# Expert rows of a mixture layer: normalized once ahead and gathered, their outputs added onto the residual rows by the scatter

## The chip, the cores and the metric

One core of one Trainium2 chip runs the whole program in one launch. The metric is device time in microseconds, here the median of several executions. The profile comes from one execution of its own and names five engines: PE (TensorE, matrix products; PEld is its weight load), DVE (VectorE), ACT (ScalarE), POOL (GpSimd) and SP (SyncE, which here only issues transfers). Data move between DRAM and the on-chip memory by DMA, issued by SP or ACT from the hardware queues, or by POOL where a row index decides the address (an indirect DMA: a gather or a scatter).

## The reference, cut to what matters

Two transformer blocks over 512 tokens of 1024 float32 features. The change lies in the end of the second block, which in the reference reads:

```python
h = h + jnp.concatenate([a_out, p_out], axis=-1) @ w_out
h = h + moe(rms_norm_2(h, ffn_norm), w_router, b_router, w_gate, b_gate, w_up, b_up, w_down, b_down)
gate = jax.nn.sigmoid(rms_norm_2(h, ple_gate_norm) @ w_ple_gate)
e = rms_norm_2(p @ w_ple_proj, ple_post_norm)
h = h + gate * e
```

In `moe` each token takes its 4 best of 32 experts (a softmax over the 4 logits gives their gates). An expert has three weights of 1024x1024 with biases: gate and up, clamped, `(up + 1) * gate * sigmoid(1.702 * gate)`, and down. The 4 results, times their gates, are summed into the token's row.

## The kernel before

The first 870 us of the profiled execution are the first block and the attention of the second, and no line of them is touched. What follows has three stages.

**Routing** (`attended_rows`, `route`), a token tile of 128 at a time, in the order 3, 2, 1, 0. The output product is added to the residual rows `hx` on DVE (`add_halves`, L855), ACT issues the store of `hx` to the DRAM tensor `base` (L1382), PE transposes `hx` and multiplies by the router, and a chain of small DVE operations makes the logits `lg` (L1314), the best four, and the table `info`: for each token and expert the row of the output to fill, the gate in two parts, the token and the row's norm in two parts. Beside it ACT and DVE split expert weights that SP loads.

**Experts**, e from 0 to 31, up to 112 tokens each (`CAP`). POOL gathers the tokens' rows of `base` into the one tile `xg` (`gather`, L1422), and normalizes them with two operations of 112x1024 (`normalize`, L1512 by the slot's norm and L1513 by the gain row; for the first expert DVE does it). PE transposes them (`flipped`, L345), ACT and DVE split them into a high and a low part. Each weight of 128x1024 is loaded by SP (L293) into a ring of slots, its high part is cast by ACT (`whi`) and its low part subtracted by DVE (`wlo`, L282). A product is three matmuls, high by high, high by low, low by high (`mm3`, L311, L312, L313), so that an expert is 144 matmuls of 512 columns, 6 for biases, 16 transposes and 4 to pick its slots: 170 instructions of PE. The activation is `gm` on ACT and `uc` on DVE. The down product of expert e-1 runs after gate and up of expert e; ACT scales its result by the gate (`yt`, L1522), and POOL scatters 112 rows of it to `ybuf` in DRAM (L1523), which holds four rows a token. Each scatter waits for the landing of the one before it.

**Last stage**, again by token tiles, after a branch (L1652) that is taken only where an expert has over 112 tokens, which does not happen here. SP loads the tile's row of `base` (`hk`), its four rows of `ybuf` (`yb`) and the embedding's rows (`ee`); DVE and POOL add the four rows to `hk` (L1703, L1705, L1706); PE transposes `hk` and multiplies by the gate's weights, loaded in eight parts `w_pg` (`gate_part`, L1576), six of them ahead of the branch. `keep_warm` puts products that nothing reads on PE, 30 behind the last down product and 24 behind the branch (L361).

A scheduler sets the order of the instructions on each engine from the dependencies, and an engine executes its own in that order.

Of the kernel before, what the change touches and what calls it, by code (L numbers as in the profile page):

```python
# [21 lines left out]
P = 128  # L22
# [93 lines left out]
class Plan:  # L116
    """Which of a set of equal slots holds each raw part of the weights, and its high and low parts.

    A stage is the parts that are multiplied at the same time, in the order of their loads: "p" is split into
    two slots, "r" is only read. ahead: how many parts are split before their stage. added: slots that come  # L120
    with a stage, behind the free ones, or from stage early on in front of them; until: the last stage of
    the slots of a pool."""

    def __init__(self, stages, slots, ahead, added=None, until=None, early=0):
# [8 lines left out]
        class State:  # L133
            # slots of each part, free slots in the order of their release, parts loaded and split
# [27 lines left out]
            def begin(st, u):  # L162
                # the splits of a stage and of those ahead of it
# [16 lines left out]
            def goes_on(st, u):  # L180
                # whether the next stages can be split without waits for their slots
# [32 lines left out]
class Piece:  # L214
    """High and low parts of columns of weights, a slot to 1024 columns."""
# [9 lines left out]
def build(tc, I, out, dbg=None, stop=None):  # L225
# [3 lines left out]
    with es:  # L229
# [28 lines left out]
        def ps_mm():  # L258
            # two banks, from one of three pairs in turn
# [17 lines left out]
        def hold(ins, after):  # L277
            # behind another instruction of its engine
# [60 lines left out]
        def transposed(xh, xT, sl, m=P, step=4):  # L339
            # [token, feature] -> feature-major high and low parts  # L340
# [16 lines left out]
        def keep_warm(n, a, b, after=None):  # L357
            # products that nothing reads: they hold the tensor engine's clock up while it has to wait
# [6 lines left out]
        # ------------------------------------------------ first block: mixer  # L365
# [24 lines left out]
        with pool("n0", 2, side="right") as n0:  # L390
# [4 lines left out]
            # values of the selected and the window branch go with the tiles of x  # L395
# [8 lines left out]
            # the gates' columns go with them  # L404
# [81 lines left out]
        def make_blocks(j, t):  # L486
# [14 lines left out]
            # high parts in the columns up to 64, low parts in those behind  # L501
# [98 lines left out]
        # branch gates  # L600
# [17 lines left out]
        with pool("gm", side="right") as gp:  # L618
            # gated mlp: its second half, normalized and mixed over the tokens of a chunk
# [40 lines left out]
        def mlp_tile(tt):  # L660
            # first half of the gated mlp, a token tile
# [208 lines left out]
        def residual_norm(pl, g_post, g_pre, h_src, h_dst, then):  # L870
            # h + rms(product), and its rms -> then(tt, h, xh)
# [27 lines left out]
        # the per-layer embedding's projection, normalized  # L899
# [36 lines left out]
        # ------------------------------------------------ first block: feed-forward  # L936
        trig = const.tile([P, 2, NT, 8], F32, name="trig")
        with pool("rope") as rp:
# [9 lines left out]
            for j, shift in enumerate((0.25, 0.0)):  # L948
                # trig[:, 0] cosine, trig[:, 1] sine, of the angle less a multiple of two pi
# [66 lines left out]
        # ------------------------------------------------ second block: mixer  # L1016
# [17 lines left out]
        # pooled half  # L1034
# [43 lines left out]
        # queries, keys and values: weights a piece ahead, work by token tiles  # L1078
# [96 lines left out]
        def diff_unit(h, qt):  # L1175
# [23 lines left out]
            def second(acc):  # L1199
# [14 lines left out]
                if h == 3 or qt == 0:  # L1214
                    # feature-major
# [36 lines left out]
        # ------------------------------------------------ second block: output product, router  # L1252
# [332 lines left out]
        for k in range(6):  # L1585
            gate_part(k)
# [160 lines left out]
```

## Time and profile before

| What | us |
|---|---|
| median of 3 runs | 2257.14 (2255.09 to 2259.49) |
| span of the profiled execution | 2253.2 |
| PE busy | 2165.2 (96%) |
| DVE busy | 1784.2 (79%) |
| ACT busy | 1374.4 (61%) |
| POOL busy | 531.7 (24%) |

The span runs from the first to the last instruction of the program in the profile; the median is 3.9 us longer. Matmuls overlap, so PE's busy time also covers short waits. In a row of the timeline the number in square brackets is the idle time of the engine just ahead of the instruction, with the instruction that ended it.

### The profile page before, as it was taken

The page shows a single profiled execution, that of the slowest core. Times are in us where ns is not written, and L with a number is a line of the kernel's source. Part 1 is how long each engine was busy: PE and PEld are TensorE (multiplying, and loading weights), DVE is VectorE, ACT ScalarE, POOL GpSimd, SP SyncE. Part 2 cuts the span into 40 slices and gives each one's busy share as a digit, 9 for nine tenths or more (in the row PEclk, how much of TensorE's full clock was granted, in tenths as well). Part 3 has the DMA queues.
Part 4 walks back from the last instruction along what each step waited for, and adds up shares of the span by engine and source line. Part 5 has one row for each costly group of instructions (what it writes and reads, how often), then busy time and mean ns, then how long its engine had stood idle before and what let it go on. Part 6 is the DMA issues. An engine that isn't in the chain of part 4 may idle for free. (4 is left out here: it accounts for less than half of the span.)

```text
span 2253.2 us, 30487 instructions
## 1 busy us (share of the span) xinstructions
PE 2165.2 (96%) x10458; PEld 1655.0 (73%) x10459; DVE 1784.2 (79%) x2583; ACT 1374.4 (61%) x1875; POOL 531.7 (24%) x391
## 2 busy tenths in 40 slices
PE   9999999999999889899999999999999999999998
PEld 7777788888888777667777777776666666666666
DVE  6688772223667676899999999999898898988876
ACT  5666652223554553577777777777676776766753
POOL 0000110000002432423131413133343533514102
PEclk9999999999999999899999999999999999999999
DMA  5411744334653036799999999999899898898836
GB/s 208 149 29 49 254 151 130 100 102 161 203 185 99 29 113 232 245 349 332 362 329 363 330 358 339 350 331 333 308 333 345 291 343 318 319 334 298 311 118 230
DMA packets 164110, 550.07 MB, mean 244 GB/s; under 512 B 23139, under 2 KB 28259, under 8 KB 163948
## 3 DMA queue, kind: packets, MB, share of 16 engines
q1 hardware_dynamic: 143520, 509.01, 63.3%
q10 hardware_dynamic: 12236, 22.25, 2.9%
q0 software_dynamic: 8192, 16.79, 2.3%
q8 instruction: 84, 1.38, 0.3%
q14 instruction: 78, 0.64, 0.1%
HBM read 534.32 MB, written 26.23 MB: 249 GB/s over the span
## 5 line engine op out<-in xcount | busy, mean ns | idle before, releaser
L282 DVE TENSOR_TENSOR wlo<-wraw,whi 128x1024 fp32r<-128x1024 f32 x923 | 1160.8, 1300 | 195.4 <-ACT whi L282 188.3
L282 ACT CAST whi<-wraw 128x1024 fp32r<-128x1024 f32 x923 | 955.4, 1053 | 389.6 <-PE pa L313 123.6
L312 PE MATMUL pa<-wlo,he 128*112 128x512 f32 x504 | 202.5, 402 | 19.8 <-DVE wlo L282 19.8
L312 PE MATMUL pb<-wlo,xe 128*112 128x512 f32 x512 | 210.3, 411 | 6.7 <-DVE wlo L282 6.4
L313 PE MATMUL pb<-whi,xe 128*112 128x512 f32 x512 | 201.3, 394 | 0.0
L313 PE MATMUL pa<-whi,he 128*112 128x512 f32 x504 | 198.2, 393 | 0.0
L311 PE MATMUL pa<-whi,he 128*112 128x512 f32 x504 | 188.9, 395 | 1.2 <-ACT he L282 1.2
L311 PE MATMUL pb<-whi,xe 128*112 128x512 f32 x512 | 186.9, 395 | 0.0
L1513 POOL TENSOR_TENSOR xg<-xg,g_ffn_norm 112x1024 f32<-112x1024 f32 x31 | 180.0, 5806 | 2.6
L1512 POOL TENSOR_SCALAR xg<-xg,slot_norm 112x1024 f32<-112x1024 f32 x31 | 141.1, 4551 | 157.8 <-DMA xg<-base,gi 157.8
L1422 POOL DMA_INDIRECT xg<-base,gi x32 | 34.2, 1069 | 608.5 <-DVE uc L1554 314.2
L317 POOL TENSOR_SCALAR rstd<-ss 128x1 f32<-128x1 f32 (+1 forms) x68 | 25.1, 369 | 622.6 <-DVE ss L862 387.3
L312 PEld LDWEIGHTS pa<-wlo,he 128*112 128x112 f32 x504 | 87.9, 174 | 57.1 <-DVE wlo L282 28.5
L312 PEld LDWEIGHTS pb<-wlo,xe 128*112 128x112 f32 x512 | 89.5, 175 | 46.1 <-DVE wlo L282 14.7
L311 PEld LDWEIGHTS pa<-whi,he 128*112 128x112 f32 x504 | 87.8, 174 | 34.9 <-ACT whi L282 4.9
L311 PEld LDWEIGHTS pb<-whi,xe 128*112 128x112 f32 x512 | 89.6, 175 | 29.5
L312 PE MATMUL pa<-wlo,xe 128*112 128x512 f32 x264 | 107.6, 407 | 2.6 <-DVE wlo L282 2.6
L311 PE MATMUL pa<-whi,xe 128*112 128x512 f32 x264 | 107.5, 407 | 0.0
L313 PEld LDWEIGHTS pb<-whi,xe 128*112 128x112 f32 x512 | 89.5, 175 | 23.6
L313 PEld LDWEIGHTS pa<-whi,he 128*112 128x112 f32 x504 | 87.9, 174 | 25.4
L313 PE MATMUL pa<-whi,xe 128*112 128x512 f32 x264 | 103.9, 394 | 0.1
L313 PE MATMUL po<-whi,xe 128*112 128x512 f32 x248 | 97.8, 394 | 0.0
(588 smaller groups left out, 4665.2 us busy)
## 6 DMA issues: line engine op xcount, KB each, us to landing
wraw<-in_we_gate_dram SPq DMA_DIRECT2D x256, 512.0 KB, 5.6
wraw<-in_we_up_dram SPq DMA_DIRECT2D x256, 512.0 KB, 5.8
wraw<-in_we_down_dram SPq DMA_DIRECT2D x256, 512.0 KB, 5.5
wraw<-in_w_gu_dram SPq DMA_DIRECT2D x44, 512.0 KB, 3.7
wraw<-in_w_down_dram SPq DMA_DIRECT2D x44, 512.0 KB, 4.3
wraw<-in_w_out_dram SPq DMA_DIRECT2D x24, 512.0 KB, 6.0
yb<-ybuf SPq DMA_DIRECT2D x6, 1024.0 KB, 12.5
wraw<-in_w_v_dram SPq DMA_DIRECT2D x10, 512.0 KB, 4.0
```

Of the source, the lines that this page charges most:

```text
L282: return nc.scalar.copy(hi, src), nc.vector.tensor_tensor(out=lo, in0=src, in1=hi.bitcast(F32), op=ALU.subtract)
L311: nc.tensor.matmul(o, a[0], b[0], start=start, stop=False)
L312: nc.tensor.matmul(o, a[0], b[1], start=False, stop=False)
L313: W["mm"] = nc.tensor.matmul(o, a[1], b[0], start=False, stop=stop)
L317: ins = nc.gpsimd.tensor_scalar(out=r[:, :w], in0=ss, scalar1=1.0 / n, scalar2=eps, op0=ALU.mult, op1=ALU.add)
L1422: nc.gpsimd.indirect_dma_start(out=xg[:CAP], out_offset=None, in_=base, in_offset=bass.IndirectOffsetOnAxis(ap=slots[e][1] if ap is None e ...
L1512: nc.gpsimd.tensor_scalar(out=xg[:CAP], in0=xg[:CAP], scalar1=slots[e][3], scalar2=None, op0=ALU.mult)
L1513: nc.gpsimd.tensor_tensor(out=xg[:CAP], in0=xg[:CAP], in1=gpre[:CAP], op=ALU.mult)
```

## The change

1. In `route` the operations that made the row of `ybuf` are gone (`e2`, `rk`, `row`), and the columns of `info` move up by one. At the end of each tile's routing DVE multiplies `hx` in place by its norm and the gain row, and ACT issues its store to a new DRAM tensor `normed`.
2. The gathers of experts 1 to 31 read `normed`, and POOL's two operations an expert are gone. Expert 0 still reads `base` and is normalized on DVE.
3. The scatter adds its rows onto `base` (an indirect DMA with an addition), in place of filling rows of `ybuf`.
4. The last stage loads `hk` in two halves and `ee` for all four tiles, without `yb` and without the additions. All eight parts of `w_pg` are loaded ahead of the branch, and the first tile's transposes go four to a group, before two.

The rest of the diff removes comments and fits the branch that is not taken.

```diff
-        ybuf = dram.tile([4 * S, D], F32, name="ybuf")
+        normed = dram.tile([S, D], F32, name="normed")
...
             if len(seen) == NT:
                 first_rows()
-            e2 = rp.tile([P, 4, NE], F32, tag="eq2", name="eq2", bufs=1)
-            nc.vector.tensor_tensor(out=e2, in0=eq, in1=row[:, tt, :, None].to_broadcast([P, 4, NE]), op=ALU.mult)
-            rk = rp.tile([P, NE], F32, tag="rk", name="rk", bufs=2)
-            nc.vector.reduce_sum(rk, e2.rearrange("p k e -> p e k"), axis=AX)
-            nc.vector.tensor_copy(info[:, tt, :, 0], rk)
...
+            scale_rows(hx, hx, r, gpre)
+            nc.scalar.dma_start(normed[tok(tt), :], hx)
...
         def gather(e, ap=None):
-            nc.gpsimd.indirect_dma_start(out=xg[:CAP], out_offset=None, in_=base, in_offset=bass.IndirectOffsetOnAxis(ap=slots[e][1] if ap is None else ap, axis=0),
+            nc.gpsimd.indirect_dma_start(out=xg[:CAP], out_offset=None, in_=normed if e else base, in_offset=bass.IndirectOffsetOnAxis(ap=slots[e][1] if ap is None else ap, axis=0),
...
-        def normalize(e):
-            if e == 0:
-                for cs in (slice(0, 512), slice(512, D)):
-                    scale_rows(xg[:CAP, cs], xg[:CAP, cs], slots[e][3], gpre[:CAP, cs])
-            else:
-                nc.gpsimd.tensor_scalar(out=xg[:CAP], in0=xg[:CAP], scalar1=slots[e][3], scalar2=None, op0=ALU.mult)
-                nc.gpsimd.tensor_tensor(out=xg[:CAP], in0=xg[:CAP], in1=gpre[:CAP], op=ALU.mult)
+        def normalize_first():
+            for cs in (slice(0, 512), slice(512, D)):
+                scale_rows(xg[:CAP, cs], xg[:CAP, cs], slots[0][2], gpre[:CAP, cs])
+
+        def add_rows(y_, ap):
+
+            nc.gpsimd.indirect_dma_start(out=base, out_offset=bass.IndirectOffsetOnAxis(ap=ap, axis=0), in_=y_, in_offset=None,
+                                         bounds_check=S - 1, oob_is_err=False, compute_op=ALU.add)
...
-            nc.gpsimd.indirect_dma_start(out=ybuf, out_offset=bass.IndirectOffsetOnAxis(ap=slots[e][2], axis=0), in_=yt, in_offset=None,
-                                         bounds_check=4 * S - 1, oob_is_err=False)
+            add_rows(yt, slots[e][1])
...
-                if kp == 1 and e + 1 < NE:
-                    normalize(e + 1)
...
-        nc.sync.dma_start(hs[0], base[tok(0), :])
...
-        for k in range(6):
+        for k in range(8):
             gate_part(k)
...
-            load_rows(0, 4)
...
+            for tt in range(NT):
+                for cs in (slice(0, 512), slice(512, D)):
+                    nc.sync.dma_start(hs[tt][:, cs], base[tok(tt), cs])
+                es.append(wp.tile([P, D], F32, name="ee", bufs=NT))
+                nc.sync.dma_start(es[tt], ed[tok(tt), :])
...
-                for cs in cols:
-                    for z in range(2):
-                        nc.vector.tensor_tensor(out=h[:, cs], in0=h[:, cs], in1=yb[:, z, cs], op=ALU.add)
-                    eng = nc.gpsimd if tt else nc.vector
-                    eng.tensor_tensor(out=yb[:, 2, cs], in0=yb[:, 2, cs], in1=yb[:, 3, cs], op=ALU.add)
-                    nc.vector.tensor_tensor(out=h[:, cs], in0=h[:, cs], in1=yb[:, 2, cs], op=ALU.add)
-                transposed(h, xT, slice(0, P), step=8 // max(parts, 2))
+                transposed(h, xT, slice(0, P), step=4)
```

On DVE, at tile 1 of the routing (`pb` is the output product that is added to this tile's residual), before:

```order
1046 L1352 TENSOR_TENSOR info<-gg,info 128x32
1047 L1318 MAX_INDEX ix<-top,lg 128x8
1048 L1342 TENSOR_SCALAR nm<-top 128x1
1049 L1320 CAST ixf<-ix 128x4
1050 L1322 TENSOR_TENSOR eq<-iota,ixf 128x128
1051 L855 TENSOR_TENSOR hx<-hx,pb 128x512
1052 L1324 TENSOR_REDUCE m<-eq 128x32
1053 L1337 TENSOR_TENSOR eq_8774<-eq,row 128x128
```

and after:

```order
1042 L1344 TENSOR_TENSOR info<-gg,info 128x32
1043 L337 SCALAR_TENSOR_TENSOR hx<-hx,rstd,g_ffn_norm_8125 128x1024
1044 L1311 SCALAR_TENSOR_TENSOR lg<-po,rstd,g_b_router_8114 128x32
1045 L855 TENSOR_TENSOR hx<-hx,pb 128x512
1046 L1314 MAX top<-lg 128x8
1047 L855 TENSOR_TENSOR hx<-hx,pb 128x512
1048 L1315 MAX_INDEX ix<-top,lg 128x8
```

The scaling in place of tile 2 (L337) now stands ahead of the additions of tile 1 (L855); it waits for the landing of tile 2's store to `base`. Tile 3's scaling stands likewise ahead of tile 2's additions, tile 1's ahead of tile 0's, and tile 0's own stands between the MAX and the MAX_INDEX of tile 0.

On POOL, the first three experts, before:

```order
252 L1422 DMA xg<-base,gi_8977 112x1024
253 L1422 DMA xg<-base,gi 112x1024
254 L1512 TENSOR_SCALAR xg<-xg,slot_norm 112x1024
255 L1513 TENSOR_TENSOR xg<-xg,g_ffn_norm_8128 112x1024
256 L1422 DMA xg<-base,gi 112x1024
```

and after:

```order
252 L1418 DMA xg<-base,gi_8965 112x1024
253 L1418 DMA xg<-normed,gi 112x1024 x3
254 L1509 DMA base<-yt,gi 512x1024
255 L1418 DMA xg<-normed,gi 112x1024
256 L1509 DMA base<-yt,gi 512x1024
```

From then on POOL has only a gather and a scatter an expert.

On SP, behind the branch (the loads of the last stage), before:

```order
568 L1668 DMA yb<-ybuf 128x4x256 x4
569 L1576 DMA wraw<-in_w_pg_dram 128x1024 x2
570 L1668 DMA hk<-base 128x1024
571 L1668 DMA yb<-ybuf 128x4x512 x2
572 L1668 DMA ee<-ed 128x1024
573 L1668 DMA hk<-base 128x1024
574 L1668 DMA yb<-ybuf 128x4x512 x2
```

and after:

```order
566 L1655 DMA hk<-base 128x512 x2
567 L1657 DMA ee<-ed 128x1024
568 L1655 DMA hk<-base 128x512 x2
569 L1657 DMA ee<-ed 128x1024
570 L1655 DMA hk<-base 128x512 x2
```

The first load of the stage is now the tile's own row, 256 KB a half, and every `hk` load comes behind the last scatters.

## Rows read from the trace of the kernel before

**Rows 1.** Busy time of each engine in two stretches of the experts; columns on top.

```profile
core 0: us, PE busy (x) PEld busy (x) DVE busy (x) ACT busy (x) POOL busy (x), PEclk, DMA share, GB/s
1200.00:1400.00 200.00, 198.70 (x902) 145.21 (x901) 196.32 (x212) 149.97 (x164) 56.40 (x22) 1.00 0.94 343
1600.00:1800.00 200.00, 192.74 (x839) 135.09 (x838) 178.94 (x199) 140.56 (x154) 76.90 (x21) 1.00 0.91 323
```

**Rows 2.** Groups of DVE and POOL, 960 to 2160: busy, mean ns, idle before.

```profile
L282 DVE TENSOR_TENSOR wlo<-wraw,whi 128x1024 fp32r<-128x1024 f32 x734 | 929.9, 1316 | 13.6 <-ACT whi L282 8.7 <-DMA wraw<-in_we_up_dram 2.1 <-DMA wraw<-in_we_gate_dram 0.3
L1555 DVE SCALAR_TENSOR_TENSOR uc<-uc,gm 112x1024 f32<-112x1024 f32 x31 | 37.7, 1216 | 0.0
...
L1513 POOL TENSOR_TENSOR xg<-xg,g_ffn_norm 112x1024 f32<-112x1024 f32 x29 | 168.0, 5794 | 2.4
L1512 POOL TENSOR_SCALAR xg<-xg,slot_norm 112x1024 f32<-112x1024 f32 x29 | 134.2, 4628 | 147.2 <-DMA xg<-base,gi 147.2
```

**Rows 3.** The same DVE group in the last expert, 2113 to 2160.

```profile
L282 DVE TENSOR_TENSOR wlo<-wraw,whi 128x1024 fp32r<-128x1024 f32 x29 | 33.8, 1218 | 1.5 <-ACT whi L282 1.5
```

**Rows 4.** Timeline, DVE and POOL at 1175: start us, us, instruction.

```profile
1174.70 4.54 DVE L282 TENSOR_TENSOR wlo<-wraw,whi 128x1024 fp32r<-128x1024 f32 x2
...
1175.53 2.64 POOL L1513 TENSOR_TENSOR xg<-xg,g_ffn_norm 112x1024 f32<-112x1024 f32 x1
```

**Rows 5.** Timeline of PE: six stalls in the experts, one with the matmul ahead.

```profile
959.46 0.49 PE L312 MATMUL pb<-wlo,xe 128*112 128x512 f32 x1 [1.96 <-DVE wlo L282]
...
993.02 0.49 PE L312 MATMUL pb<-wlo,xe 128*112 128x512 f32 x1 [1.08 <-DVE wlo L282]
...
1182.02 0.40 PE L311 MATMUL pb<-whi,xe 128*112 128x512 f32 x1
1182.63 0.48 PE L312 MATMUL pb<-wlo,xe 128*112 128x512 f32 x1 [0.21 <-DVE wlo L282]
...
1750.30 0.49 PE L312 MATMUL pa<-wlo,he 128*112 128x512 f32 x1 [0.65 <-DVE wlo L282]
...
1764.92 0.49 PE L312 MATMUL pa<-wlo,xe 128*112 128x512 f32 x1 [0.15 <-DVE wlo L282]
...
2001.70 0.49 PE L312 MATMUL pa<-wlo,he 128*112 128x512 f32 x1 [1.66 <-DVE wlo L282]
```

**Rows 6.** Timeline of DVE in the routing: additions of tiles 2 and 1, one reduction.

```profile
877.57 1.38 DVE L855 TENSOR_TENSOR hx<-hx,pa 128x512 f32<-128x512 f32 x2 [0.77 <-PE pa L313]
...
890.02 0.68 DVE L855 TENSOR_TENSOR hx<-hx,pb 128x512 f32<-128x512 f32 x1
...
905.25 0.37 DVE L1339 TENSOR_REDUCE rk<-eq 128x32 f32<-128x128 f32 x1
```

**Rows 7.** Stores to base issued at 878.98, 890.73 and 898.05: KB, us to landing.

```profile
base<-hx ACTq DMA_DIRECT2D x1, 512.0 KB, 9.4
...
base<-hx ACTq DMA_DIRECT2D x1, 512.0 KB, 8.5
...
base<-hx ACTq DMA_DIRECT2D x1, 512.0 KB, 2.6
```

**Rows 8.** Timeline of POOL: the first expert's gather.

```profile
908.60 1.57 POOL L1422 DMA_INDIRECT xg<-base,gi  x1 [7.41 <-DVE most L1360]
```

**Rows 9.** Scatters, us to landing: the last one, and those from 960 to 2160.

```profile
ybuf<-yt,si POOLq DMA_INDIRECT x1, 3.7
...
ybuf<-yt,si POOLq DMA_INDIRECT x30, 7.2
```

**Rows 10.** Timeline of PE in the last stage: warm products, first matmuls of tiles.

```profile
2188.14 5.72 PE L361 MATMUL tr<-whi 128*128 128x512 f32 x24 [1.41 <-PEq L1652]
...
2194.98 0.50 PE L311 MATMUL pb<-whi,x4T 128*128 128x512 f32 x1 [0.46 <-ACT x4T L282]
...
2223.75 0.50 PE L311 MATMUL pa<-whi,x4T 128*128 128x512 f32 x1 [1.56 <-ACT x4T L282]
...
2236.39 0.50 PE L311 MATMUL pb<-whi,x4T 128*128 128x512 f32 x1 [0.38 <-ACT x4T L282]
```

More of the change, by code (lines that the diff above doesn't have):

```diff
@@ L1259, in build @@
         nc.vector.tensor_copy(iota, iota_i)
-        row_i = mixq.tile([P, NT, 4], I32, name="row_i")
-        row = mixq.tile([P, NT, 4], F32, name="row")
-        nc.gpsimd.iota(row_i, pattern=[[4 * P, NT], [1, 4]], base=0, channel_multiplier=4)
-        nc.vector.tensor_copy(row, row_i)
         tok1_i = mixq.tile([P, NT], I32, name="tok1_i")
@@ L1429, in first_rows @@
             for tt in range(NT):
-                nc.tensor.matmul(pt[:CAP, 0:2], oh0[0][:, tt], info[:, tt, 0, 3:5], start=tt == 0, stop=tt == NT - 1)
+                nc.tensor.matmul(pt[:CAP, 0:2], oh0[0][:, tt], info[:, tt, 0, 2:4], start=tt == 0, stop=tt == NT - 1)
             gi = early.tile([P, 2], I32, name="gi0", bufs=1)[:CAP]
@@ L1528, in build @@
         held = (W["gate"], first)
-        normalize(0)
+        normalize_first()
         prepare_slots(1, 1)
@@ L1569, in build, with gate_part @@
         hs = [row_tile("hk") for _ in range(NT)]
[L1570 removed]
         wpg = []
[L1573 removed]
+        def gate_part(k):
             slot, *pair = W["plan"].next()
             raw = slot_tile(slot, F32, "wraw")
[L1576 to L1578 removed]
+            nc.sync.dma_start(raw, I["w_pg"][k // 2][:, (k % 2) * D:(k % 2 + 1) * D])
             hi, lo = [slot_tile(t, F32R, n) for t, n in zip(pair, ("whi", "wlo"))]
@@ L1661, in build @@
         with pool("fin", 2, side="right") as wp:
-            yv = ybuf.rearrange("(t k) d -> t k d", k=4)
             keep_warm(24, wpg[0][0][:, 0:P], wpg[0][0][:, 0:512])
-            es, ybs = {}, {}
-            chain = []
-            def load(dst, src):
-                ins = nc.sync.dma_start(dst, src)
-                if chain and len(chain) < 9:
-                    hold(ins, chain[-1])
-                chain.append(ins)
-            def load_rows(tt, parts):
-                ybs[tt] = wp.tile([P, 4, D], F32, name="yb")
-                for c in range(parts):
-                    cs = slice(c * D // parts, (c + 1) * D // parts)
-                    load(ybs[tt][:, :, cs], yv[tok(tt), :, cs])
@@ L1679, in load_row @@
-            def load_row(tiles, tt, src):
-                if tt not in tiles:
-                    tiles[tt] = wp.tile([P, D], F32, name="ee")
-                load(tiles[tt], src[tok(tt), :])
-            load_rows(0, 4)
-            for k in range(6, 8):
-                gate_part(k, chain[-1])
-            hs = dict(enumerate(hs))
-            load_row(hs, 1, base)
-            load_rows(1, 2)
-            load_row(es, 0, ed)
-            for tt in range(NT):
-                parts = 4 if tt == 0 else 2
-                cols = [slice(c * D // parts, (c + 1) * D // parts) for c in range(parts)]
-                if tt + 2 < NT:
-                    load_row(hs, tt + 2, base)
-                    load_rows(tt + 2, 2)
-                if tt + 1 < NT:
-                    load_row(es, tt + 1, ed)
-                h, e, yb = hs[tt], es[tt], ybs[tt]
-                xT = [wp.tile([P, 8, P], F32R, name=f"x4T{j}") for j in range(2)]
-                for cs in cols:
-                    for z in range(2):
-                        nc.vector.tensor_tensor(out=h[:, cs], in0=h[:, cs], in1=yb[:, z, cs], op=ALU.add)
-                    eng = nc.gpsimd if tt else nc.vector
-                    eng.tensor_tensor(out=yb[:, 2, cs], in0=yb[:, 2, cs], in1=yb[:, 3, cs], op=ALU.add)
-                    nc.vector.tensor_tensor(out=h[:, cs], in0=h[:, cs], in1=yb[:, 2, cs], op=ALU.add)
-                transposed(h, xT, slice(0, P), step=8 // max(parts, 2))
```

47 lines of the change are left out of this document (22 added, 25 removed).

## The prediction, made before the changed kernel was run

> **What bounds the kernel now.** I read the busy times by stretch first. The experts, from about 940 to 2180 us, are over half of the span, and they run in two regimes [rows 1]. Between 1200 and 1400 PE is busy for 198.70 of 200 us with 902 matmuls; an expert of 170 instructions takes 170 x 200 / 902 = 37.7 us, and no engine but PE can set that. DVE stands beside it with 196.32 us, so it has hardly any slack of its own. Between 1600 and 1800 PE has 192.74 us and 839 matmuls, which is 40.5 us an expert, although DVE has only 178.94. So the second regime loses some 2.8 us an expert to the order of the instructions, not to anyone's total work. Second I read the timeline of PE for its stalls: each ends on `wlo`, the low part that DVE makes [rows 5]. Third I asked what makes `wlo` late. Over all experts one takes 1316 ns in the mean [rows 2], in the last expert, which has no normalization of POOL beside it, 1218 ns [rows 3]. At 1174.70 two of them take 4.54 us where two alone would take 2.44, and POOL's L1513 of 2.64 us lies beside them [rows 4]. POOL's two operations therefore cost DVE (1316 - 1218) x 734 = 72 us over 29 experts, 2.5 us each. DVE time is not the bound; what counts is the PE stall that it leads to.
>
> **The change part by part.**
>
> *POOL's normalization, removed.* I go by stalls, since PE is the bound. In the first regime one stall an expert falls behind the blocked pair: the matmul at 1182.63 starts 0.61 us after the one ahead, where the pitch of all instructions is 198.70 / 902 = 0.22 and I take 0.23 for a full matmul; 0.38 us lost, 0.21 of it shown as idle, so a stall costs some 0.17 more than its idle time [rows 1, 5]. There are 11 such experts, with nearly the same stall, from 1068.8 to 1448.4: -4.2 us. In the second regime most of the loss is not POOL's: at 1750.30 PE waits 0.65 us for a `wlo` that stands on DVE behind the activation `uc`, and there the order is unchanged. What POOL does there is the stall at 1764.92, 0.15 of idle and so 0.32 lost; 13 experts, -4.2. One expert of this regime has a stall of 1.66 at 2001.70 beside POOL; -1.7. The first experts have two large ones, 1.96 at 959.46 and 1.08 at 993.02; -3.0 if both are POOL's, -1.1 if the first is also a late weight. POOL's removed time itself (5.79 + 4.63 us an expert [rows 2]) is off the path and counts for nothing. The gather then feeds the transposes directly and only has more time. The order of PE turns into the second regime one expert earlier: between 0 and +2.8, I take half, +1.3. Sum of the experts: -11.8, between -5 and -17.
>
> *The Trainium skill, "SBUF — State Buffer", section "Who interferes with whom", has a rule for this: a DVE instruction with two inputs there and a GpSimd instruction that reads it exclude each other, and the second is blocked until the first ends. By the rule DVE would lose all of POOL's 10.4 us an expert. The trace has 2.5 us, so it agrees only in part, and the rows decide the sum; by the rule the sum would be that of the second rival below, 2233.8.*
>
> *Scaling in place and second store in the routing, added.* Four scalings of 128x1024, near in kind to `uc` (1216 ns [rows 2]), and four more stores of 512 KB on ACT's queue. The point is where they stand on DVE: in order ahead of the next tile's additions, and waiting for the landing of that tile's own store to `base`, which is read from the same rows. Queued behind the waiting instruction on DVE are the additions, the routing chain and the splits; behind its store on ACT stand the next tile's store to `base` and the exponentials. Step by step: tile 3's scaling delays tile 2's additions, which ended at 878.95, by 1.2 to 2; their store goes at about 880.5 in place of 878.98. It lands 9.4 later [rows 7] at 889.9; tile 2's scaling ends at 891.1; tile 1's two additions of 0.69 with two small operations between end at 892.9, before at 890.70 [rows 6]: +2.2. That store takes 8.5 (901.4), tile 1's scaling ends at 902.7, tile 0's additions at 904.4 against a store at 898.05: +6.3. If it lands in 2.6 as the last one did [rows 7], this wait falls away and +2.2 stays; I take 8.5, since it is the time of the store at the same place. Tile 0's own scaling stands inside its routing chain, +1.2, while three small operations leave it, the longest 0.37 [rows 6], about -0.8 as an estimate. Its store, landing in 2.6, is done by then; in 8.5 it would hold the chain for some 4 more. So the first gather, at 908.60 [rows 8], is late by 6.5, between +2.5 and +10.5. PE has nothing to do before it, and the ring of split weights is full, so nothing later pays it back.
>
> *Scatter that adds.* No row shows an accumulating transfer. In the experts it is hidden: a scatter lands in 7.2 us [rows 9], the next waits for it an expert, 37.7 us, later, and its source rows have further buffers. At the end the last scatter is issued ahead of the branch, so before 2188.14 - 1.41 = 2186.7, and a plain one lands in 3.7 [rows 9, 10], by 2190.4; warm products hold PE until 2193.86 in any case. Twice the time would expose 0 to 3 us. I take 0, since a row of 112 tokens is small, and keep +3.
>
> *The Trainium skill, "DMA: Bandwidth & Descriptors", section "Rules for kernel authors", speaks against this part: an accumulating DMA reads its destination and writes it later, and nothing holds the bytes in between. By it the loads of `hk` cannot pass the last scatter, and each row crosses twice. No run here shows it; by that rule the sum would move by the +3 just named.*
>
> *Last stage.* 8 MB of `yb` loads and all additions go. The start cannot move forward, as the 24 warm products run from 2188.14 for 5.72 us [rows 10]; eight transposes ahead of the first matmul in place of two make it about 0.4 later. The first two tiles take 2223.75 - 2194.98 = 28.8 us, the third 12.64 [rows 10]; with the adds gone both should run like the third: 2 x 12.64 = 25.3, so -3.5. Together -3.1, between 0 and -5. The two more gate parts ahead of the branch are split by ACT and DVE while PE runs the warm products, and their cover is that wait; without it they would cost two `wlo`, 2.4 us.
>
> **Sum.** +6.5 - 11.8 - 3.1 = -8.4. The profiled execution would have a span of 2244.8 in place of 2253.2; the median lies 3.9 above the span, so 2248.7.
>
> **The rivals.**
>
> *No relief.* The stalls of PE come from the order on DVE alone, as at 1750.30 [rows 5], and when POOL is gone another wait for `wlo` stands there. For: DVE has 196.32 of 200 us in the first regime [rows 1]. Against: the last expert without POOL has shorter splits [rows 3]. Then +6.5 + 1.3 - 3.1 = +4.7: 2261.8.
>
> *Full relief.* DVE, freed of 2.5 us or more, runs ahead so far that the second regime loses no idle time of PE: 7.26 of 200 us, 1.47 an expert, 13 experts, -19 in place of -4.2 [rows 1]. Then 2233.8. Against: `uc` waits for PE whatever POOL does.
>
> *Stores behind stores (slower).* On ACT's queue each store to `base` now follows a store to `normed` of the same size. If the two share the queue's time, a landing takes 9.4 longer at tiles 2 and 1, and DVE waits each time: +18.8, net +10.4, 2267.5. It decides from 4.2 us more a landing, where the gain is gone. For: 9.4 and 8.5 show a loaded DMA. Against: 2.6 for the last one [rows 7].
>
> *Accumulating scatter as the bound (slower).* The DMA share is 0.94 in the first regime [rows 1], 6% or 2.3 us an expert free. If an adding scatter takes the engines 7.2 us longer, 4.9 us an expert would show, 31 times: +152, 2401. It decides at 2.3 us.
>
> **How the numbers follow.** Chances: the forecast 0.50, no relief 0.18, full relief 0.10, stores behind stores 0.14, the scatter 0.08 (half of it only the +3 of the end). A measurement tells about 0.2%, 4.5 us, from no change. The forecast with its own spread is faster by that in 0.40 and the same in 0.10; full relief is faster; no relief stands at the edge, 0.12 same, 0.06 slower; stores 0.03 and 0.11; scatter 0.03 and 0.05. So faster 0.50, same 0.28, slower 0.22. The range 2236 to 2266 reaches from near full relief to nearly the slow stores and leaves out the bad scatter.
>
> **What would show it.** Right: `wlo` at 1.22 in the mean, no stall of PE above 0.3 where L1512 stood, first regime at 37.3 us an expert, first gather at 915, tiles of the last stage 12.6 apart. Wrong: a first gather near 909 or beyond 920, stalls of PE that stay, landings of scatters above 15 us, or a second regime that begins elsewhere.

## The result

The changed kernel takes 2236.43 us (median of 4 runs, 2233.82 to 2238.70) against 2257.89 us before (median of 4 runs): a ratio of 0.9906, with a 95% interval of 0.9892 to 0.9920. It is 21.5 us faster, where 8.4 were forecast. The direction was right and the size was not. The time lies 0.4 us inside the lower end of the range. One execution each of two later kernels, of 5307.8 and 3457.2 us, is left out of their times below.

The span of the profiled execution is 2235.0 us, 18.2 less than before. The 3 us between this and the medians lie between executions. A span is some 1.7 us shorter than the time of its execution (2235.0 and 2236.76 here), so the profiled one of before took about 2255 us, 2.9 below its median, and this one lies 0.3 above. I cut the span at the first and the last activation of the experts, the `gm` row on ACT.

Before, the timeline of ACT (start, length, instruction):

```profile
943.58 1.06 ACT L1553 ACTIVATE gm<-gm 112x1024 f32<-112x1024 f32 x1 [0.40 <-DVE gm L1552]
...
2152.20 1.06 ACT L1553 ACTIVATE gm<-gm 112x1024 f32<-112x1024 f32 x1 [4.94 <-DVE gm L1552]
```

After, the same two:

```profile
945.18 1.06 ACT L1547 ACTIVATE gm<-gm 112x1024 f32<-112x1024 f32 x1
...
2133.70 1.06 ACT L1547 ACTIVATE gm<-gm 112x1024 f32<-112x1024 f32 x1 [4.96 <-DVE gm L1546]
```

| Stretch | before | after | moved | forecast |
|---|---|---|---|---|
| up to the first activation | 943.6 | 945.2 | +1.6 | +6.5 |
| first to last activation | 1208.6 | 1188.5 | -20.1 | -11.8 |
| last activation to the end | 101.0 | 101.3 | +0.3 | -3.1 |
| span | 2253.2 | 2235.0 | -18.2 | -8.4 |

In these two executions all of the gain lies in the experts. The page of the changed kernel, its busy times and its costliest group:

```profile
PE 2156.0 (96%) x10458; PEld 1658.2 (74%) x10459; DVE 1699.7 (76%) x2475; ACT 1372.4 (61%) x1873; POOL 199.2 (9%) x323
...
L282 DVE TENSOR_TENSOR wlo<-wraw,whi 128x1024 fp32r<-128x1024 f32 x923 | 1096.7, 1221 | 226.7 <-ACT whi L282 209.8
```

The low part `wlo` takes 1221 ns in the mean over the whole kernel, which is what it took alone [rows 3]. By stretch:

```profile
core 0: us, PE busy (x) PEld busy (x) DVE busy (x) ACT busy (x) POOL busy (x), PEclk, DMA share, GB/s
1200.00:1400.00 200.00, 200.00 (x909) 147.46 (x908) 186.96 (x202) 152.85 (x167) 13.90 (x11) 1.00 0.95 347
1600.00:1800.00 200.00, 193.67 (x851) 137.17 (x850) 172.28 (x190) 142.06 (x156) 12.42 (x10) 1.00 0.91 327
```

In the first regime PE is busy for all of the 200 us and gets through 909 instructions in place of 902; in the second it is 851 in place of 839 [rows 1]. Where the stall stood that delayed a matmul to 0.61 us behind the one ahead [rows 5], 21.3 us behind the activation, PE's timeline now reads:

```profile
1177.42 0.40 PE L313 MATMUL pb<-whi,xe 128*112 128x512 f32 x1
1177.66 0.39 PE L311 MATMUL pb<-whi,xe 128*112 128x512 f32 x1
1177.89 0.40 PE L312 MATMUL pb<-wlo,xe 128*112 128x512 f32 x1
1178.12 0.39 PE L313 MATMUL pb<-whi,xe 128*112 128x512 f32 x1
```

The pitch, the time from start to start, is 0.23 us throughout. In the routing the forecast waits are there, on DVE:

```profile
877.47 1.29 DVE L337 SCALAR_TENSOR_TENSOR hx<-hx,rstd,g_ffn_norm 128x1024 f32<-128x1024 f32 x1 [1.15 <-DMA base<-hx]
...
888.03 1.28 DVE L337 SCALAR_TENSOR_TENSOR hx<-hx,rstd,g_ffn_norm 128x1024 f32<-128x1024 f32 x1 [2.75 <-DMA base<-hx]
...
898.33 1.28 DVE L337 SCALAR_TENSOR_TENSOR hx<-hx,rstd,g_ffn_norm 128x1024 f32<-128x1024 f32 x1 [2.77 <-DMA base<-hx]
```

Each scaling waits for the landing of its tile's store, and the first gather goes at 913.65 on POOL, 5.05 us later than before [rows 8]:

```profile
913.65 1.28 POOL L1418 DMA_INDIRECT xg<-base,gi  x1 [9.31 <-DVE gi L1430]
```

### The profile page after: what moved, and what is told of

It is laid out like the page before. It is cut to its first block, busy times and chain, and to the rows that moved or that the text cites. A ratio compares the mean times of both kernels' runs of the same rounds, so it can differ in the third digit from the quotient of the medians.

```text
span 2235.0 us, 30297 instructions
## 1 busy us (share of the span) xinstructions
PE 2156.0 (96%) x10458; PEld 1658.2 (74%) x10459; DVE 1699.7 (76%) x2475; ACT 1372.4 (61%) x1873; POOL 199.2 (9%) x323
## 5 line engine op out<-in xcount | busy, mean ns | idle before, releaser
L282 DVE TENSOR_TENSOR wlo<-wraw,whi 128x1024 fp32r<-128x1024 f32 x923 | 1096.7, 1221 | 226.7 <-ACT whi L282 209.8
L1509 POOL DMA_INDIRECT base<-yt,gi x32 | 47.7, 1489 | 567.7 <-DVE wlo L282 461.9
L313 PE MATMUL po<-whi,xe 128*112 128x512 f32 x248 | 97.7, 394 | 0.0
L312 PE MATMUL po<-wlo,xe 128*112 128x512 f32 x248 | 97.6, 394 | 0.0
L311 PE MATMUL po<-whi,xe 128*112 128x512 f32 x248 | 97.4, 393 | 0.0
L1418 POOL DMA_INDIRECT xg<-normed,gi x31 | 33.5, 1081 | 600.0 <-PE tr L345 570.2
```

Source lines behind the costliest of these rows:

```text
L282: return nc.scalar.copy(hi, src), nc.vector.tensor_tensor(out=lo, in0=src, in1=hi.bitcast(F32), op=ALU.subtract)
L311: nc.tensor.matmul(o, a[0], b[0], start=start, stop=False)
L312: nc.tensor.matmul(o, a[0], b[1], start=False, stop=False)
L313: W["mm"] = nc.tensor.matmul(o, a[1], b[0], start=False, stop=stop)
L1418: nc.gpsimd.indirect_dma_start(out=xg[:CAP], out_offset=None, in_=normed if e else base, in_offset=bass.IndirectOffsetOnAxis(ap=slots[e][1 ...
L1509: nc.gpsimd.indirect_dma_start(out=base, out_offset=bass.IndirectOffsetOnAxis(ap=ap, axis=0), in_=y_, in_offset=None, bounds_check=S - 1, ...
```

## The theories and the experiments

Three questions were open. Why did the experts gain 20 us and not 12: POOL's operations alone (A), or the order of PE's instructions, which changed in some experts (C)? The sizes of the forecast are B. Why did a gather that is 5 us late cost only 1.6? And where did the last stage's gain go?

**POOL's two operations left out of the kernel before.** Nothing else is changed, and the matmuls stand in the order of before.

```diff
-                nc.gpsimd.tensor_scalar(out=xg[:CAP], in0=xg[:CAP], scalar1=slots[e][3], scalar2=None, op0=ALU.mult)
-                nc.gpsimd.tensor_tensor(out=xg[:CAP], in0=xg[:CAP], in1=gpre[:CAP], op=ALU.mult)
+                pass
```

> The kernel before, with POOL's two operations an expert (L1512, L1513) left out and nothing else: experts 1 to 31 then work on rows that are not normalized, so this part of the computation is missing. The order of the matmuls is that of before, expert by expert. Theory A, POOL's reads block DVE's splits and each late split stops PE: from the first activation of an expert to the last the time falls from 1208.6 us by 18 to 20, as in the changed kernel (1188.6), and the wide stalls of PE ahead of a low part (0.61 us in the first regime, 0.55 in the second, 1.96 and 1.08 in the first experts, 1.66 at 2001) are gone. Theory B, the sizes of the prediction: about -12. Theory C, what changed the experts is the other order of the instructions in the changed kernel: -4 or less.

Measured: 2236.41 us, ratio 0.9903 (0.9876 to 0.9929). Its two activations on ACT:

```profile
943.92 1.06 ACT L1552 ACTIVATE gm<-gm 112x1024 f32<-112x1024 f32 x1
...
2132.47 1.06 ACT L1552 ACTIVATE gm<-gm 112x1024 f32<-112x1024 f32 x1 [4.94 <-DVE gm L1551]
```

The experts take 1188.55 us, as in the changed kernel, though the order is that of before. Theory A holds to a tenth of a microsecond, C falls, and so do the sizes of the forecast (B). The changed kernel also has two small DVE operations an expert fewer, `slot_norm` and `si`, of some 0.15 us each; this kernel still has both, so they are worth nothing that shows.

**The two operations put back into the changed kernel**, first both, then each alone.

```diff
+                if kp == 1 and e + 1 < NE:
+                    nc.gpsimd.tensor_scalar(out=xg[:CAP], in0=xg[:CAP], scalar1=1.0, scalar2=None, op0=ALU.mult)
+                    nc.gpsimd.tensor_tensor(out=xg[:CAP], in0=xg[:CAP], in1=gpre[:CAP], op=ALU.mult)
```

> The changed kernel, with two operations of POOL back at their old place, on the gathered rows: a multiplication by 1.0 and one by the gain row (so the gain is applied twice, which is the only change of the computation). The order of the matmuls is that of the changed kernel. Theory A: the experts take 1188.6 + 18 to 20 us again, and the whole some 18 to 20 us more than the changed kernel. Theory B: +12. Theory C (order): +4 or less.

> The changed kernel, with one operation of POOL an expert back, the multiplication by 1.0 (one tensor read, one written); the result is that of the changed kernel. With both operations back the experts took 1224.7 us, against 1188.5 without. Theory F: what blocks DVE is POOL's operation with two tensors read; this one alone costs 0 to 5 us over the experts. Theory G: any operation of POOL that reads costs by its length; this one has about half of the 36 us.

> The changed kernel, with the other operation of POOL an expert back, the product with the gain row (two tensors read), so that the gain is applied twice. Theory F: 15 to 36 us over the experts against 1188.5. Theory G: about half of the 36 us, 12 to 20. Under both the stall of PE is largest where the operation lies beside the splits that follow the activation.

| Kernel | experts, us | time, us |
|---|---|---|
| changed kernel | 1188.5 | 2236.4 |
| multiplication by 1.0 back | 1195.7 | 2244.6 (one run) |
| product with the gain row back | 1224.4 | 2273.0 (one run) |
| both back | 1224.7 | 2274.6 (2259.0 to 2287.8) |

Both operations back cost 36 us, not the 18 to 20 that A expected from the kernel before: the direction held, the size did not. The costs of the two do not add up either, and the kernel's runs scatter by 29 us. The product with the gain row alone has nearly all of it, as F said, so G falls; the multiplication costs 7, a little more than F's 0 to 5 and all of it in the second regime. The place of the blocked instruction explains most of this. In the kernel with the product back, at 1754, on POOL, DVE and PE:

```profile
1754.04 3.94 POOL L1544 TENSOR_TENSOR xg<-xg,g_ffn_norm 112x1024 f32<-112x1024 f32 x1 [4.02 <-DMA xg<-normed,gi]
...
1754.52 1.21 DVE L282 TENSOR_TENSOR wlo<-wraw,whi 128x1024 fp32r<-128x1024 f32 x1
1755.65 3.42 DVE L1551 SCALAR_TENSOR_TENSOR uc<-uc,gm 112x1024 f32<-112x1024 f32 x1
...
1759.75 1.10 PE L345 MATMUL tr<-ident,uc 112*128 112x112 f32 x8 [2.31 <-DVE xe L282]
```

POOL's operation does not slow the split beside which it begins; the next one, the activation `uc`, takes 3.42 us in place of 1.22, until 1.1 us behind the end of POOL's, and PE, which has its transposes right behind, stands for 2.31. In the kernel with the multiplication back, at 1702:

```profile
1701.64 2.96 POOL L1544 TENSOR_SCALAR xg<-xg 112x1024 f32<-112x1024 f32 x1 [5.35 <-DMA xg<-normed,gi]
...
1701.89 2.06 DVE L1551 SCALAR_TENSOR_TENSOR uc<-uc,gm 112x1024 f32<-112x1024 f32 x1
...
1704.63 1.11 PE L345 MATMUL tr<-ident,uc 112*128 112x112 f32 x8 [0.95 <-DVE xe L282]
```

Here `uc` takes 2.06 and ends at 1703.95, ahead of POOL's end at 1704.60. So one DVE operation an instruction of POOL is held, for about 2.2 us by the product of two tensors and 0.85 by the multiplication by a number, and the price is set by what PE waits for at that moment: 0 where a split has lead, 0.4 to 0.5 in the first regime, over 2 where `uc` is hit. The gather's landing decides which one is hit, as it releases POOL. The one expert of before with 1.66 us at 2001.70 [rows 5] is the same thing, not an accident. There POOL's multiplication starts 5.4 us behind the activation, in the experts next to it 3.5 and 3.7, and the product holds the third `wlo` behind the splits `xe`, so that these four take 7.07 us:

```profile
1995.71 7.07 DVE L282 TENSOR_TENSOR wlo<-wraw,whi 128x1024 fp32r<-128x1024 f32 x4
...
1997.92 2.65 POOL L1513 TENSOR_TENSOR xg<-xg,g_ffn_norm 112x1024 f32<-112x1024 f32 x1
```

A part of the 36 us is the clock and not the block itself. Behind the stall at 1759.75 PE's granted clock (the column behind POOL's) fell to its lower level, 1.2 GHz, in the kernel with the product back:

```profile
core 0: us, PE busy (x) PEld busy (x) DVE busy (x) ACT busy (x) POOL busy (x), PEclk, DMA share, GB/s
1757.00:1759.00 2.00, 0.44 (x2) 0.00 (x0) 2.00 (x2) 1.30 (x2) 0.99 (x1) 1.00 0.62 238
1763.00:1765.00 2.00, 2.00 (x6) 1.46 (x5) 2.00 (x3) 0.80 (x1) 0.00 (x0) 0.50 0.84 266
```

It did so four times in the experts in each of the two profiles with the product back, and never in those of before or of the changed kernel. In the kernel with the product alone, an expert in which `uc` was hit took 43.8 us where the clock fell and 41.9 to 42.3 where it did not. At some 1.6 us each, the four make an estimated 6 of the 36 us. Whether they also make the scatter of the runs is not shown.

**The scaled rows in a tile of their own**, in the changed kernel.

```diff
-            scale_rows(hx, hx, r, gpre)
-            nc.scalar.dma_start(normed[tok(tt), :], hx)
+            nx = rp.tile([P, D], F32, tag="nx", name="nx", bufs=2)
+            scale_rows(nx, hx, r, gpre)
+            nc.scalar.dma_start(normed[tok(tt), :], nx)
```

> The changed kernel, with the scaled rows in a tile of their own, so that DVE no longer waits for the landing of the store to base. Theory D, the wait is what delays the routing: the three waits of 1.15, 2.75 and 2.77 us on DVE ahead of the scalings vanish, the first gather goes at 909 to 910 in place of 913.65, and the first activation comes 1 to 3 us earlier than 945.2; the whole gains 1 to 3 us. Theory E, the delay is absorbed by then (the gather lands faster when it goes later, and PE's first matmuls run at the full clock): the first gather is earlier but the first activation is at 944 to 946 and the whole is unchanged within 1 us.

> The kernel with the scaled rows in a tile of their own once more, beside the others on one chip: 2229 to 2231 us, 5 to 7 us faster than the changed kernel (2236.4), with no wait of DVE for a store ahead of a scaling and the first activation at 938 to 941.

Measured: 2230.11 us, ratio 0.9882 (0.9853 to 0.9910), and once more 2231.01, ratio 0.9892 (0.9876 to 0.9909). By the medians it is 5.4 to 6.3 us faster than the changed kernel. The intervals of the ratios overlap with that of the changed kernel (0.9892 to 0.9920), so the traces have to decide. Its timeline, of DVE, POOL and ACT:

```profile
883.78 1.27 DVE L337 SCALAR_TENSOR_TENSOR nx<-hx,rstd,g_ffn_norm 128x1024 f32<-128x1024 f32 x1
...
892.93 1.28 DVE L337 SCALAR_TENSOR_TENSOR nx<-hx,rstd,g_ffn_norm 128x1024 f32<-128x1024 f32 x1
...
908.08 1.28 POOL L1419 DMA_INDIRECT xg<-base,gi  x1 [8.43 <-DMA wraw<-in_we_gate_dram]
...
939.09 1.06 ACT L1548 ACTIVATE gm<-gm 112x1024 f32<-112x1024 f32 x1
```

No scaling waits for a store, the gather goes 5.6 us earlier than in the changed kernel, and the first activation comes 6.1 us earlier. Of this, 1.0 us was there ahead of the routing; 5.0 remain. The second profile has no such wait either, and its first activation, at 940.8, is 5.8 us ahead of that in the second profile of the changed kernel (946.6). Theory D holds, with a gain of 5 to 6 us where it said 1 to 3; E falls. The routing's delay was never absorbed: without the waits the first activation comes 2.8 to 4.5 us earlier than before (943.6), a gain that has another source, and the waits took more than that.

**The first two parts of the change alone, and second profiles.** The kernel before, with the rows scaled in place, stored, and gathered from there, POOL's operations gone, and the scatter and the last stage of before.

```diff
+            scale_rows(hx, hx, r, gpre)
+            nc.scalar.dma_start(normed[tok(tt), :], hx)
...
-            nc.gpsimd.indirect_dma_start(out=xg[:CAP], out_offset=None, in_=base, in_offset=bass.IndirectOffsetOnAxis(ap=slots[e][1] if ap is None else ap, axis=0),
+            nc.gpsimd.indirect_dma_start(out=xg[:CAP], out_offset=None, in_=normed if e else base, in_offset=bass.IndirectOffsetOnAxis(ap=slots[e][1] if ap is None else ap, axis=0),
```

> The kernel before, with the first two parts of the change alone: rows scaled in place at the end of the routing and stored to the new tensor, experts 1 to 31 gathered from there, POOL's operations gone; the scatter still fills the four rows a token and the last stage is that of before. If the last stage and the scatter gave nothing in sum (the trace has +0.2 us from the last activation to the end), this is as fast as the changed kernel within 3 us, about 2236 to 2240. If they did give the 3 us of the prediction, it is 2240 to 2243. The routing should delay the first gather to about 914.

> The kernel before with the first two parts of the change alone, for a second profile. The first one had the first gather at 914.3, its landing 8.9 us later, and the first activation at 950.2, and its time, 2242.5, was the longest of its four runs (2233.75 to 2242.5). Theory I: the first activation is 2 to 6 us earlier this time, as the clock comes back earlier. Theory J: the landing is 8 to 9 us again and the first activation at 948 to 951.

> The changed kernel once more, for a second profile. In the first one the first activation of the experts came at 945.2 although the first gather went at 913.65, 5 us later than before. Theory I, the routing's delay is passed on, and how much of it shows depends on the execution, by the landing of the first gather (6.6 us against 8.8 before) and by the time at which PE's clock comes back (922.3 in the first profile, 930.2 in that of the kernel with the first two parts alone): the second profile has the gather at 913 to 915 again, but the first activation anywhere from 944 to 951. Theory J, this kernel's gather lands early by its order: the landing is 6 to 7 us again, and the first activation within 1 us of 945.2. In both the experts take 1188.5 us.

Measured: 2236.01 us, ratio 0.9897 (0.9870 to 0.9924), the same as the changed kernel within the scatter of the runs (2233.75 to 2242.51). What the adding scatter and the short last stage are worth is too small for the medians. By the profiles in which the clock stayed up, the time from the last activation to the end is 99.5 us in the changed kernel (the second one) and 99.6 and 99.3 with the own tile, against 101.0 before, 101.1 without POOL's operations and 101.6 here: some 1.5 to 2 us, which one fall of the clock takes away again, as in the first profile of the changed kernel. The first activation here came at 950.2 in the first profile, 6.6 us later than before, and at 945.2 in the second, where the gather went at 910.2 in place of 914.3. The changed kernel's came at 945.2 and 946.6. The landing of the first gather did not move between executions: 8.9 us in both profiles of this kernel, 8.8 before and 8.3 without POOL's operations, but 6.6 and 6.1 in the changed kernel, 6.1 and 6.4 with the own tile. Theory J holds for the landing, and I for the rest: the time of the gather moves by 4 us from one execution to the next. Of these 4 us, 2.4 lie ahead of the routing, and the rest in the waits of the scalings, 3.6 us in sum in the first profile and 1.8 in the second.

**The addition taken out of the scatter**, in the changed kernel.

```diff
-                                         bounds_check=S - 1, oob_is_err=False, compute_op=ALU.add)
+                                         bounds_check=S - 1, oob_is_err=False)
```

> The changed kernel, with scatters that write their rows in place of adding them (the sum over a token's experts and its residual is left out, so the last stage works on other rows). Theory H: the addition makes the last scatter land late (POOL has it 7.3 us behind the last down product, where a plain one took 5.1), the branch and the warm products behind it start later, PE idles 2.3 us and its clock falls for 3.4 us. Then without the addition POOL has it at 5.1, the warm products start at 8.5 in place of 9.5, the first product of the last stage comes 15 to 16 us behind the last down product in place of 18.0, and the whole gains 1 to 3 us. Rival: the loads of the rows themselves hold the start, and it gains under 0.5 us. In the experts nothing changes either way (1188.5 us).

Measured: 2234.68 us, ratio 0.9898 (0.9873 to 0.9924), some 1.8 us faster than the changed kernel by the medians, within the spread of the runs; the traces tell more. PE in the changed kernel, from the last down product on:

```profile
2161.01 0.39 PE L313 MATMUL po<-whi,he 128*112 128x512 f32 x1
2161.24 6.97 PE L361 MATMUL tr<-whi 128*128 128x512 f32 x30
2170.55 7.33 PE L361 MATMUL tr<-whi 128*128 128x512 f32 x24 [2.33 <-PEq L1641]
2177.72 1.04 PE L345 MATMUL tr<-ident,hk 128*128 128x128 f32 x8
2179.00 0.50 PE L311 MATMUL pb<-whi,x4T 128*128 128x512 f32 x1 [0.24 <-ACT x4T L282]
...
2193.74 0.50 PE L313 MATMUL pa<-whi,x4T 128*128 128x512 f32 x1 [0.86 <-DVE x4T L282]
```

and without the addition:

```profile
2160.83 0.39 PE L313 MATMUL po<-whi,he 128*112 128x512 f32 x1
2161.06 6.97 PE L361 MATMUL tr<-whi 128*128 128x512 f32 x30
2169.53 5.73 PE L361 MATMUL tr<-whi 128*128 128x512 f32 x24 [1.49 <-DVE wlo L1573]
2175.10 1.04 PE L345 MATMUL tr<-ident,hk 128*128 128x128 f32 x8
```

The last scatter lands in 5.8 us with the addition and in 3.7 without, as before [rows 9]. POOL waits for it behind the branch, until 7.3 us behind the last down product with the addition and 5.1 without. With it, PE comes out of the branch only after that; without it, a low part on DVE ends PE's wait. PE's idle time is 2.33 us with and 1.49 without. In this execution the clock then fell to its lower level, 1.2 GHz, for 3.4 us, so that the 24 warm products took 7.33 in place of 5.73, as the stretches of the changed kernel show (the column behind POOL's is PE's granted clock):

```profile
core 0: us, PE busy (x) PEld busy (x) DVE busy (x) ACT busy (x) POOL busy (x), PEclk, DMA share, GB/s
2168.00:2171.00 3.00, 0.67 (x3) 0.44 (x3) 2.56 (x3) 0.74 (x1) 0.00 (x0) 1.00 0.02 6
2171.00:2175.00 4.00, 4.00 (x13) 3.09 (x12) 0.00 (x0) 0.17 (x1) 0.00 (x0) 0.58 0.88 276
```

Theory H holds for the start: the first product of the last stage comes 15.5 us behind the last down product without the addition, 18.0 with it, and 16.2 in the second profile of the changed kernel, where the clock stayed up. So the addition itself costs some 0.7 us here and the fall of the clock the rest. The idle time alone does not tell whether the clock falls: it stayed up behind 1.84 us in that second profile and behind 1.98 with the own tile, and fell behind 1.81 in the kernel with both operations back.

**Two versions of the last stage**, both from the kernel with the own tile: other numbers of warm products, and the next tile's rows split ahead of this tile's last products.

```diff
-        keep_warm(30, wpg[0][0][:, 0:P], wpg[0][0][:, 0:512], last)
+        keep_warm(33, wpg[0][0][:, 0:P], wpg[0][0][:, 0:512], last)
...
-            keep_warm(24, wpg[0][0][:, 0:P], wpg[0][0][:, 0:512])
+            keep_warm(18, wpg[0][0][:, 0:P], wpg[0][0][:, 0:512])
```

> The kernel with the scaled rows in a tile of their own, with 33 warm products in place of 30 behind the last down product and 18 in place of 24 behind the branch. PE's idle time between them falls from 2.0 to about 1.3 us, the clock stays up, and the first transposes of the last stage follow the landing of their rows (about 12.8 us behind the last down product) in place of the warm products (14.75). Expected: first product of the last stage 15.0 to 15.5 us behind the last down product in place of 16.2, the whole 0.5 to 1.5 us faster than the kernel it is made from. If the rows land later than that, nothing changes.

Measured: 2229.45 to 2233.62 us in four runs, ratio 0.9878 (0.9853 to 0.9903), no different from the kernel it is made from. No profile shows the place in question as it is in these runs, so this stays open.

```diff
+            def flip_rows(tt):
+                xTs[tt] = [wp.tile([P, 8, P], F32R, name=f"x4T{j}") for j in range(2)]
+                transposed(hs[tt], xTs[tt], slice(0, P), step=4)
...
+                if tt + 1 < NT:
+                    flip_rows(tt + 1)
                 for c0, c1 in groups:
```

> The kernel with the scaled rows in a tile of their own, with the transposes and splits of the next tile's rows written ahead of this tile's last products on DVE in the last stage. In the changed kernel tile 1's matmuls stop 0.86 us for a split that stands on DVE behind four operations of tile 0, and the tile takes 13.8 us in place of 12.6. Expected: the split stands behind two of them, the last stage from its first to its last product 49.6 to 50.0 us in place of 50.5, the whole 0.5 to 1 us faster than the kernel it is made from. If ACT's sigmoids ahead of the split are what is late, nothing changes.

Measured: 2229.08 us, ratio 0.9886 (0.9869 to 0.9902), the shortest median of all, though its interval overlaps that of the kernel it is made from. On DVE at tile 1:

```profile
2184.11 1.33 DVE L1684 TENSOR_TENSOR sgm<-sgm,ee 128x512 f32<-128x512 f32 x2 [10.26 <-ACT sgm L1683]
2185.36 1.28 DVE L282 TENSOR_TENSOR x4T<-tr,x4T 128x512 fp32r<-128x512 f32 x2
2186.56 1.28 DVE L1685 TENSOR_TENSOR sgm<-sgm,hk 128x512 f32<-128x512 f32 x2
```

The splits stand ahead of the second pair, and the last stage takes 49.3 us from its first to its last product in place of 50.5: the 0.86 us at 2193.74 above are gone.

## Why the prediction was right in kind and wrong in size

The step that failed is the size of one term, POOL's normalization: -11.8 us was forecast, and -20.1 came. The stretch ahead of the experts cost less than forecast (+1.6 in place of +6.5) and the last stage gave less (+0.3 in place of -3.1). These two misses partly cancel, and the span moved by -18.2 where -8.4 was forecast.

*What bounds the kernel.* Right. An expert of the first regime took 37.95 us from activation to activation, not the 37.7 counted from instructions, and takes 37.5 now (forecast 37.3). PE bounds both regimes, the stalls end on DVE's low parts, and POOL is the cause of those that went; the stall at 1750.30 that I put down to the order is still there in the second regime, 1.13 us from start to start.

*POOL's normalization.* Right in mechanism, mis-sized: -20.1 in place of -11.8, and the kernel without the two operations alone has all of it. "0.38 us lost" an expert in the first regime was 0.48. I left out that the matmul behind a stall is late too, by 0.09: the one at 1182.63 [rows 5] is followed by

```profile
1182.95 0.40 PE L313 MATMUL pb<-whi,xe 128*112 128x512 f32 x1
```

which is 0.32 us to the next start in place of 0.23. 11 experts gave -5.2, not -4.2. In the second regime "0.15 of idle and so 0.32 lost" was about 0.5 in each of the 13 experts; with the one at 2001.70, which gave -2.2 in place of -1.7, they gave -8.8, where I had -5.9. The first three gave -5.3 and not -3.0: from rows of idle time I counted two stalls, while from start to start they are larger and smaller ones stand between. The step "the order of PE turns into the second regime one expert earlier, +1.3" was too large: those two experts gave -0.7, and -1.1 in the order of before without POOL's operations, so the order cost 0.4. Summing idle times row by row was the weak method. The last expert of before, the only one without POOL beside it, would have been the better yardstick, start by start.

*The rule on reads that exclude each other.* I set POOL's recorded 10.4 us an expert against it and found that it agreed in part. The rows above show the flaw: POOL's recorded time contains its own waiting (the product has 2.64 us at least and 9.70 at most), so it was no measure of the block. For the product, one instruction of DVE is held until POOL's has ended, 2.2 us; there the trace agrees with the Trainium skill, "SBUF — State Buffer", section "Who interferes with whom". For the multiplication by a number it agrees only in part: the hold is 0.85 us, and the held `uc` ends 0.65 us ahead of POOL's instruction.

*Scaling in place.* The waits are as forecast, by place and nearly by length: the first gather late by 5.05 us (forecast 6.5). Counted from the start of the routing it is 4.5 and 6.2 us later than in the kernel with the own tile, by the first and the second profiles. "Nothing later pays it back" was right as well, since that kernel won 5 to 6 us. What I missed is a gain ahead of the experts that the scaling has no part in: the gather lands 2.2 us sooner, one stall of 0.4 ahead of the first activation was POOL's, and PE's clock is back at the first matmul (922.3 and 922.7), where before it came back 2 us behind it (921.8 and 919.7). Before, PE stood idle ahead of the transposes of the gathered rows:

```profile
918.21 1.74 PE L345 MATMUL tr<-ident,xg 112*128 112x112 f32 x8 [2.85 <-DVE xg L337]
```

In the changed kernel they follow the warm products without a gap, since the rows land at 920.2, ahead of the end of the warm products at 921.2 (before, 917.4 and 915.4). Net +1.6 in this execution, and +3.0 in the second profile.

*The scatter that adds.* "I take 0 and keep +3" failed at its end: the landing took 2.1 us more, and the wait for it showed. I had followed the loads of `hk`, which were not late, but not the branch, where PE waits for POOL and POOL for the scatter.

*The last stage.* "-3.5 with the adds gone" was -2.3: tiles 0, 1 and 2 start 12.7, 13.8 and 12.6 us apart, and tile 1 stands 0.86 us for a split that DVE reaches only behind tile 0's last products. "About 0.4 later" for its start was 2.5 in this execution, 0.8 in the second profile. From the last activation to the end the sum was +0.3 here and -1.5 there, for a forecast of -3.1.

*The rivals.* No relief did not come: the six kernels without POOL's operations agree on the experts within 0.7 us. Stores behind stores did not come: in the kernel without the addition, which has the changed kernel's routing, the four stores to `base` land in 6.4, 6.8, 8.7 and 3.2 us, before in 6.3, 9.4, 8.5 and 2.6. The scatter as the bound did not come: the experts take 1188.5 us with the addition and without it. Full relief has a time, 2233.8, near the 2236.4 measured, but by luck: it named -19 in the second regime, where -8.8 came and the loss at 1750.30 stayed. I gave that case 0.10, because I took the stalls that I could see for all that there were.

## What to carry to other kernels

An engine that is busy a quarter of the time and on no path can still set the time: what counts is whom it blocks, and whether that one has lead at that moment. Measure such a loss as the difference of two whole periods, with and without, rather than as a sum of visible idle times. And an operation in place on rows that a store still reads makes the engine wait for the store: a second buffer was worth 5 to 6 us here, where the whole change gave 21.5.

## What the hardware showed that was not expected

A product of two tensors on POOL holds one two-input operation of DVE for 2.2 us, a multiplication by a number for 0.85. The clock can make a stall dearer: behind one of 2.31 us it fell to 1.2 GHz. Beside back-to-back splits POOL itself is the one that waits, up to 9.7 us for 2.6 of work. An adding scatter of 112 rows of 4 KB at the end lands in 5.4 to 5.8 us where a plain one takes 3.7, and in the experts in 8.3 in the median, against 7.2 before and 6.9 in the changed kernel without the addition. The first gather lands in 6.1 to 6.6 us in the kernels with the short routing table and in 8.3 to 8.9 in those with the long one; weight loads that are issued beside it differ, but no run told this cause from others, and it stays open.
